# Expert layers of a two-layer trunk: where the third split buffer starts, and when the first expert blocks are split

## The chip, the cores and the metric

The kernel runs on one core of one Trainium2 chip. The metric is device time in microseconds (us) of one execution; lower is better. A core has TensorE (PE, matrix products), VectorE (DVE), ScalarE (ACT) and GpSimd (POOL), each with a queue of its own that it works through in order, and SyncE (SP), which only issues transfers here. Engines wait for each other through semaphores alone.

## The reference, cut to what matters

Two layers run over 640 tokens (128 of a prompt, 512 of a sample) of width 1024. Each layer has a mixer and then an expert stage, and the expert stage is where the change lies:

```python
q = (xc @ w_q).reshape(PEER_CHUNK, PEER_HEADS, 2, half)
s = jnp.einsum('thpc,hpnc->thpn', q, sub_keys)
sv, si = lax.top_k(s, PEER_TOPK)                  # 16 of 128, per token, head and half
cand = sv[..., 0, :, None] + sv[..., 1, None, :]
fv, fi = lax.top_k(cand.reshape(...), PEER_TOPK)  # 16 of the sums
gates = jax.nn.softmax(fv, axis=-1)
act = jax.nn.gelu(jnp.einsum('thkd,td->thk', u[eidx], xc))
y = jnp.einsum('thk,thkd->td', gates * act, v[eidx])
```

There are 16384 experts, so `u` and `v` are 16384 x 1024 each. For the sample the kernel doesn't gather: it computes all the products with `u`, and multiplies by a dense matrix of gates, and then all the products with `v`.

## The kernel before, in words

**Products in three passes.** A float32 product is made of three matmuls on rounded operands: with `hi` the rounded operand and `lo` the rest, hi·hi, hi·lo and lo·hi. The activations are split once (`hh`, `hl`). Each weight tile, 128 x 1024, is loaded to `wr` (`w_load`, line 277, on SP; 3 buffers), its high half `wh` is rounded on ScalarE (`w_hi`, line 294), and its low half `wl` is the difference, on line 303 (`w_lo`), on VectorE, or on GpSimd for tiles marked "g". `mm3` (line 361) issues the matmuls; with the order of `PAIRS`, the third matmul of a block is the first that reads `wl`.

**The order of the weights.** `seq` lists all weight tiles in the order of their use; for a layer's expert stage these are 16 query tiles `w_q` ("g"), 128 blocks of `u` and 128 blocks of `v` (both "v"). `w_get(ahead)` (line 341) hands out the next tile. Before that it splits tiles until `ahead` tiles from this one on are split, and asks for loads up to three further on:

```python
while st["split"] < min(i + ahead, len(seq)):
    w_split()
while st["load"] < min(i + 1 + AHEAD, len(seq)):
    w_load()
```

What stands in these loops goes into the queues of ScalarE, VectorE (or GpSimd) and SP at that point of the program; there is no other scheduler in the stretches that the change touches.

**Buffers of split tiles.** `wh` and `wl` have two buffers each (`WB`). `EXTRA` names tiles that go elsewhere: the third to fifth query tile, counted from 0 the tiles 2 to 4, have their own, and every third tile from 18 on (that is, from block 2 of `u`) takes a third buffer, `wh3` and `wl3` (lines 1267 to 1269). A split waits until the matmuls that read its buffer's former tile are done.

**The query chunks.** `peer` (line 1258) first plans the normalisation with the products of chunks 0 to 2 (`plan.run`, line 1368). Chunks 3 to 15 are a loop written out by hand (lines 1377 to 1387): `w_get()` with `ahead=2`, 48 matmuls of 320 columns, a copy of the result on ScalarE, and `score(c - 1)` for the chunk before: five matmuls against the keys on TensorE (line 1327), two copies on ScalarE (lines 1335 and 1333), and five calls of `top16` on VectorE (lines 1189 to 1193; called a search below), one for each 128 tokens. `s5` has 3 buffers, `q` has 2. `score(15)` ends the stage. Tile 16, which is block 0 of `u`, is split by the `w_get` of chunk 15.

**The blocks of `u`.** The loop from line 1532 runs over 128 blocks: `w_get(3)`, 24 matmuls of 512 columns into a new PSUM bank (`pu_`), a Gelu on ScalarE and a store. The rest of the routing goes between the blocks, step by step: `background()` (line 1429) yields its cost, and the loop spends a credit on it that grows by 4.6 a block:

```python
credit = min(credit + 4.6, 6.0)
while credit > 0 and alive:
    cst = next(bg, None)
```

The credit starts at -10. The steps are the second top-16, the softmax, one-hot operands for groups of four tokens (lines 1464 and 1466) and their matmuls (lines 1410 and 1411). From the prompt's routing on each block also takes one product of a gathered row with the prompt (`dot`, line 1397), and two when the background is through. When it is, and nothing of it is on its way, other pools open (`open_late`, line 1481); then each block takes a step of layer 1's modulation (line 189; in layer 0 only, 96 steps), and eight blocks each load a part of the dense gates (line 1504).

**The blocks of `v`.** The loop from line 1603 runs over 128 blocks, 24 matmuls each (line 1618), with one gathered row added for the prompt (line 1596), and modulation steps in five of eight blocks.

Of the kernel before, what the change touches and what calls it, by code (L numbers as in the profile page):

```python
# [28 lines left out]
NB = 128  # L29
# [127 lines left out]
def tile_trunk(ctx: ExitStack, tc: tile.TileContext, a, o):  # L157
# [110 lines left out]
    st = {"load": 0, "split": 0, "get": 0}  # L268
# [3 lines left out]
    def w_load():  # L272
        i = st["load"]
        if i < len(seq):
            ap, K, M, _ = seq[i]
            r = pw.tile([128, 1024], F32, name="wr", tag="wr", bufs=3)
            SP.dma_start(r[:, :K * M], ap if K == 1 else ap.rearrange("p k m -> p (k m)"))
            RAW[i] = r
            st["load"] += 1

    def w_hi():
        i = st["split"]
        while st["load"] <= i:
            w_load()
        _, K, M, eng = seq[i]
        n = K * M
        if i in EXTRA:
            hi, lo = EXTRA.pop(i)
            if callable(hi):
                hi, lo = hi(), lo()  # L290
        else:
            hi = pw.tile([128, 1024], F32R, name="wh", tag="wh", bufs=WB)
            lo = pw.tile([128, 1024], F32R, name="wl", tag="wl", bufs=WB)
        S.activation(hi[:, :n], RAW[i][:, :n], AF.Copy)  # L294
        SPLIT[i] = (hi, lo)
        st["split"] += 1
        return i

    def w_lo(i, eng=None):
        _, K, M, e = seq[i]  # L300
        n = K * M
        hi, lo = SPLIT[i]
        (eng or (V if e == "v" else G)).tensor_tensor(lo[:, :n], RAW.pop(i)[:, :n], hi[:, :n],  # L303
                                                      op=OP.subtract)

    def w_split():
        if st["split"] < len(seq):
            w_lo(w_hi())
# [32 lines left out]
    def w_get(ahead=2):  # L341
        i = st["get"]
        st["get"] += 1
# [4 lines that stand above are left out]
        _, K, M, _ = seq[i]  # L348
        hi, lo = SPLIT.pop(i)
        if K == 1:  # L350
            return hi, lo
        return (hi[:, :K * M].rearrange("p (k m) -> p k m", k=K),
                lo[:, :K * M].rearrange("p (k m) -> p k m", k=K))
# [3 lines left out]
    def mm3(outs, L, R, K, order=None):  # L357
        for i, k in enumerate(order or range(K)):
            for n, (x, y) in enumerate(PAIRS):
                for h, out in enumerate(outs):  # L360
                    PE.matmul(out, L[x](k), R[y](k, h), start=(i == 0 and n == 0),  # L361
                              stop=(i == K - 1 and n == 2))
# [10 lines left out]
    def wcol(t):  # L373
        return lambda k: t[:, k, :]
# [811 lines left out]
    def top16(v16, ix, s5, c, tt):  # L1186
        sc = s5[:, tt]
        v, x = v16[:, tt, c], ix[:, tt, c]
        V.max(v[:, 0:8], sc)  # L1189
        V.max_index(x[:, 0:8], v[:, 0:8], sc)  # L1190
        V.match_replace(sc, v[:, 0:8], sc, -3e38)  # L1191
        V.max(v[:, 8:16], sc)  # L1192
        V.max_index(x[:, 8:16], v[:, 8:16], sc)  # L1193
# [64 lines left out]
    def peer(l, A, B, gt):  # L1258
        act_d = pd.tile([NB - NR, 128, TS], F32, name=f"act_d{l}")
        g_d = pd.tile([128, TS // GC, NB, GC], F32, name=f"g_d{l}")  # L1260
        with tc.tile_pool(name="pg", bufs=1) as pg:
# [2 lines left out]
            aP = pg.tile([128, 128], F32, name="aP")  # L1264
            idx = pg.tile([128, 128], I32, name="idx")
            gat = {}
            for i in range(st["get"] + 18, st["get"] + 16 + 2 * NB, 3):
                EXTRA[i] = tuple((lambda n=n: pg.tile([128, 1024], F32R, name=n, tag=n, bufs=1))
                                 for n in ("wh3", "wl3"))

# [16 lines left out]
            with tc.tile_pool(name="ph", bufs=1) as tmp, \  # L1287
# [29 lines left out]
                def copy_q(ps):  # L1317
                    q = tmp.tile([128, T], F32, name="q", tag="q", bufs=2)
                    S.activation(v2(q), ps[:, :, :HT], AF.Copy)
                    return q  # L1320

                def score_mm(c, s5, part):
                    q = qs[c]
                    pa = p_mm.tile([128, 512], F32, name="psa", tag="s", bufs=2)
                    for t in range(4 * part, 4 + part):
                        n = (t % 4) * 128
                        PE.matmul(pa[:, n:n + 128], q[:, t * 128:(t + 1) * 128], keys[:, c], start=True,
                                  stop=True)
                    return pa

                def score_copy(s5, part, pa):
                    if part:
                        S.activation(s5[:, 4], pa[:, :128], AF.Copy)
                    else:
                        S.activation(s5[:, 0:4], pa.rearrange("p (t n) -> p t n", t=4), AF.Copy)

                def s5_tile():
                    return tmp.tile([128, 5, 128], F32, name="s5", tag="s5", bufs=3)
# [31 lines left out]
                def score(c):  # L1370
                    s5 = s5_tile()
                    for part in range(2):
                        score_copy(s5, part, score_mm(c, s5, part))
                    for t in range(5):
                        top16(v16, ix, s5, c, t)

                for c in range(2, 16):
                    if c == 2:
                        ps = firsts[c][0]
                    else:  # L1380
                        hi, lo = w_get()
                        ps = p_mm.tile([128, 2, 512], F32, name="pp", tag="mm", bufs=3)
                        mm3([ps[:, h, :HT] for h in range(2)], (wcol(hi), wcol(lo)), RH, KD)
                    qs[c] = copy_q(ps)
                    if c > 2:
                        score(c - 1)
                score(15)

            pps = late.enter_context(tc.tile_pool(name="pps", bufs=1, space=PSUM))
# [82 lines left out]
                            yield "grp"  # L1472

            bg = background()
            credit = -10.0
            ndot = [0, False]
            alive = True
            opened = []
# [53 lines left out]
            for i in range(NB):  # L1532
                hi, lo = w_get(3)
# [19 lines left out]
                credit = min(credit + 4.6, 6.0)  # L1553
# [49 lines left out]
            for n in range(NB):  # L1603
                hi, lo = w_get(1)
# [55 lines left out]
    with tc.tile_pool(name="tmp", bufs=1) as tmp, tc.tile_pool(name="pmm", bufs=1, space=PSUM) as p_mm:  # L1660
# [146 lines left out]
        mixer0(p_mm, tmp, gt, firsts)  # L1807
    A, B, gt = norm_cols(0, 1)
    peer(0, A, B, gt)
    mod_finish(1, 0, 48)  # L1810
    A, B, gt = norm_cols(1, 0)
    with tc.tile_pool(name="tmp", bufs=1) as tmp, tc.tile_pool(name="pmm", bufs=1, space=PSUM) as p_mm:
        mixer1(p_mm, tmp, A, B, gt)
    A, B, gt = norm_cols(1, 1)
    peer(1, A, B, gt)
    with tc.tile_pool(name="tmp", bufs=1) as tmp, tc.tile_pool(name="pmm", bufs=1, space=PSUM) as p_mm:
        plan = Plan()
# [118 lines left out]
```

## Time and profile before

| what | us |
|---|---|
| median of 3 runs | 3701.89 |
| lowest and highest run | 3700.79, 3709.65 |
| the profiled execution | 3704.95 |
| its span in the trace | 3703.2 |
| TensorE busy in the span | 3581.9 |
| VectorE busy | 2976.3 |
| ScalarE busy | 1644.4 |
| GpSimd busy | 656.2 |

The profile is of one execution of the program; its times start at the first instruction. A row in order of time has the start, the duration, the engine, the line, the operation with the tile written and the tiles read, and, where the engine stood idle before it, for how long and what ended that. Rows of the waits sum such idle time by who waited for whom. The clock of a stretch is the share of TensorE's full clock (2.4 GHz) that was granted in it. A run of like instructions is put together in one row, with a count. The expert stage of layer 0 runs from about 358 to 1990 us, that of layer 1 from about 2056 us to the end of its blocks.

### The profile page before, as it was taken

What the parts mean: (1) busy time and instruction counts of PE and PEld (TensorE: products, weight loads), DVE (VectorE), ACT (ScalarE), POOL (GpSimd) and SP (SyncE); (2) the same over time, 40 slices, a digit from 0 to 9 for tenths busy, and PEclk for the clock granted to TensorE, in tenths of its full rate; (3) what the DMA queues carried; (4) which work ended last, traced back from release to release, by engine and by line L of the source; (5) the groups of instructions that cost most, each with busy time, mean ns of one, the idle gap of its engine ahead of it and who ended that gap; (6) DMA issues with size and microseconds to landing.
All of it is one profiled execution on the core that took longest, in us unless ns stands there. A gap on an engine that the chain in (4) does not pass through costs nothing. (4 is left out here: it accounts for less than half of the span.)

```text
span 3703.2 us, 52825 instructions
## 1 busy us (share of the span) xinstructions
PE 3581.9 (97%) x18190; PEld 2980.4 (80%) x18190; DVE 2976.3 (80%) x6989; ACT 1644.4 (44%) x2904; POOL 656.2 (18%) x564
## 2 busy tenths in 40 slices
PE   8998989999999999999996889999999999999998
PEld 6957978888888888888885888888888888888886
DVE  8967889898997788888887898998989656666665
ACT  6743324756757333333333423757657333333332
POOL 0000112111111322222210111111111412222220
PEclk9999999999999999999998999999999999999999
DMA  5243126888878999999991215878888978888883
GB/s 206 80 138 118 60 77 222 285 260 271 280 257 288 367 324 331 326 323 321 324 313 40 77 54 194 278 256 289 262 266 278 341 262 295 296 295 298 299 295 116
DMA packets 400162, 894.58 MB, mean 242 GB/s; under 512 B 33746, under 2 KB 170386, under 8 KB 399252
## 3 DMA queue, kind: packets, MB, share of 16 engines
q1 hardware_dynamic: 272884, 490.07, 41.3%
q0 software_dynamic: 74016, 271.09, 21.4%
q10 hardware_dynamic: 52992, 130.05, 9.0%
q8 instruction: 142, 2.33, 0.3%
q14 instruction: 128, 1.05, 0.1%
HBM read 758.26 MB, written 132.81 MB: 241 GB/s over the span
## 5 line engine op out<-in xcount | busy, mean ns | idle before, releaser
L303 DVE TENSOR_TENSOR wl<-wr,wh 128x1024 fp32r<-128x1024 f32 (+2 forms) x556 | 665.7, 1198 | 518.7 <-ACT wh L294 448.3
L294 ACT ACTIVATE wh<-wr 128x1024 fp32r<-128x1024 f32 (+1 forms) x578 | 601.8, 1042 | 930.7 <-PE po L1618 734.2
L1274 POOL DMA_INDIRECT gat<-in_u_dram,idx x256 | 289.1, 1129 | 1258.6 <-DVE oh L1464 642.8
L1618 PE MATMUL po<-wgl,wh 128*128 128x512 f32 x2032 | 501.8, 389 | 0.0
L1618 PE MATMUL po<-wgh,wh 128*128 128x512 f32 x2032 | 501.8, 389 | 0.0
L1618 PE MATMUL po<-wgh,wl 128*128 128x512 f32 x2032 | 501.8, 389 | 0.0
L1274 POOL DMA_INDIRECT gat<-in_v_dram,idx x256 | 303.6, 1186 | 1016.3 <-DVE accP L1596 957.4
L1618 PEld LDWEIGHTS po<-wgh,wl 128*128 128x128 f32 x2032 | 381.5, 188 | 79.1
L1618 PEld LDWEIGHTS po<-wgl,wh 128*128 128x128 f32 x2032 | 381.5, 188 | 79.1
L1618 PEld LDWEIGHTS po<-wgh,wh 128*128 128x128 f32 x2032 | 381.5, 188 | 79.1
L1596 DVE SCALAR_TENSOR_TENSOR accP<-gat,aP,accP 128x1024 f32<-128x1024 f32 x254 | 324.8, 1279 | 0.5
L1397 DVE SCALAR_TENSOR_TENSOR gat<-gat,hP 128x1024 f32<-128x1024 f32 x256 | 311.0, 1219 | 15.0 <-DMA gat<-in_u_dram,idx 14.9
L1466 DVE TENSOR_SCALAR oh<-iota,ij,gs 128x128 f16<-128x128 f16 x1024 | 322.0, 314 | 0.0
L1405 ACT ACTIVATE oh<-oh,gs 128x128 f16<-128x128 f16 x1024 | 316.5, 387 | 0.0
L1528 ACT ACTIVATE wgh<-w 128x512 fp32r<-128x512 f32 x256 | 161.9, 632 | 208.0 <-PE po L1618 205.8
L1464 DVE TENSOR_SCALAR oh<-iota,ij 128x128 f16<-128x128 f16 x1024 | 253.2, 247 | 0.0
L1530 DVE TENSOR_TENSOR wgl<-w,wgh 128x512 fp32r<-128x512 f32 x256 | 174.9, 683 | 8.7 <-ACT wgh L1528 8.7
L1417 ACT ACTIVATE stag<-pgm 128x512 f32<-128x512 f32 x256 | 135.5, 579 | 0.0
L1410 PE MATMUL pgm<-oh 128*128 128x128 f16 x1024 | 129.4, 220 | 0.0
L1411 PE MATMUL pgm<-oh 128*128 128x128 f16 x1024 | 128.1, 219 | 0.0
L189 DVE SCALAR_TENSOR_TENSOR mjunk<-wm,silu 128x1024 f16<-128x1024 f32 x96 | 117.0, 1218 | 11.0 <-DMA gt__12579<-g_d 9.1
L1410 PEld LDWEIGHTS <-oh 128*128 128x128 f16 x1024 | 96.9, 98 | 33.5 <-DVE oh L1464 23.3
(2260 smaller groups left out, 6989.3 us busy)
## 6 DMA issues: line engine op xcount, KB each, us to landing
wr<-in_uT_dram SPq DMA_DIRECT2D x256, 512.0 KB, 4.5
wr<-in_v_dram SPq DMA_DIRECT2D x256, 512.0 KB, 4.5
g_d<-stag ACTq DMA_DIRECT2D x128, 512.0 KB, 6.4
act_d<-at ACTq DMA_DIRECT2D x240, 256.0 KB, 4.8
at<-act_d SPq DMA_DIRECT2D x240, 256.0 KB, 4.8
wm<-in_w_mod_dram SPq DMA_DIRECT2D x88, 512.0 KB, 7.2
hl<-g_d SPq DMA_DIRECT2D x128, 256.0 KB, 5.6
wr<-in_w_q_dram SPq DMA_DIRECT2D x32, 512.0 KB, 3.6
```

Source lines behind the costliest of these rows:

```text
L294: S.activation(hi[:, :n], RAW[i][:, :n], AF.Copy)
L303: (eng or (V if e == "v" else G)).tensor_tensor(lo[:, :n], RAW.pop(i)[:, :n], hi[:, :n], op=OP.subtract)
L1274: G.indirect_dma_start(out=r, out_offset=None, in_=a[f"u{l}" if s < 128 else f"v{l}"], in_offset=bass.IndirectOffsetOnAxis(ap=idx[:, s % 1 ...
L1397: V.scalar_tensor_tensor(ug, ug, 1.0, hP, op0=OP.mult, op1=OP.mult, accum_out=aP[:, s:s + 1])
L1405: S.activation(oh[:, 2], oh[:, 1], AF.Copy, scale=gr[:, tl:tl + 1])
L1410: PE.matmul(pgm[:, n], oh[:, 0], oh[:, 1], start=True, stop=False)
L1464: V.tensor_scalar(oh[:, 0], iota16, ij[:, 1, tl:tl + 1], None, op0=OP.is_equal)
L1466: V.tensor_scalar(oh[:, 1], iota16, ij[:, 0, tl:tl + 1], gs[:, 0, tl:tl + 1], op0=OP.is_equal, op1=OP.mult)
L1528: S.activation(wh, w32, AF.Copy)
L1530: return lambda: V.tensor_tensor(wl, w32, wh, op=OP.subtract)
L1596: V.scalar_tensor_tensor(accP, vg, aP[:, s:s + 1], accP, op0=OP.mult, op1=OP.add)
L1618: PE.matmul(po[d], (hi, lo)[x][:, d * 128:(d + 1) * 128], (wh, wl)[y], start=(n == 0 and p == 0), stop=False)
```

## The change

The third buffer pair is used from tile 7 on, every third tile (7, 10, 13, then 16, which is block 0 of `u`, and so on), in place of from tile 18 on. The chunks' `w_get` keeps three tiles split from the one in use, in place of two. Ahead of `score(15)` a loop splits until three tiles beyond chunk 15 are split. The credit of the background work starts at -14.

```diff
-            for i in range(st["get"] + 18, st["get"] + 16 + 2 * NB, 3):
+            for i in range(st["get"] + 7, st["get"] + 16 + 2 * NB, 3):
                 EXTRA[i] = tuple((lambda n=n: pg.tile([128, 1024], F32R, name=n, tag=n, bufs=1))
                                  for n in ("wh3", "wl3"))
...
                     else:
-                        hi, lo = w_get()
+                        hi, lo = w_get(3)
                         ps = p_mm.tile([128, 2, 512], F32, name="pp", tag="mm", bufs=3)
...
                     if c > 2:
                         score(c - 1)
+                while st["split"] < st["get"] + 3:
+                    w_split()
                 score(15)
...
             bg = background()
-            credit = -10.0
+            credit = -14.0
```

## Rows read from the trace of the kernel before

**Rows 1.** TensorE in the page's first part: busy us, share of the span, instructions

```profile
PE 3581.9 (97%) x18190; PEld 2980.4 (80%) x18190; DVE 2976.3 (80%) x6989; ACT 1644.4 (44%) x2904; POOL 656.2 (18%) x564
```

**Rows 2.** waits of TensorE, whole span: us in total, times, longest

```profile
PE pu__20832 L361 <- DVE wl L303: 10.8, 1, 10.8
PE pu__4604 L361 <- DVE wl L303: 10.8, 1, 10.8
...
PE pu__20798 L361 <- DVE wl L303: 3.1, 1, 3.1
PE pu__4570 L361 <- DVE wl L303: 3.0, 1, 3.0
...
PE pt__21555 L1445 <- DVE fj L1255: 1.8, 1, 1.8
```

**Rows 3.** stretches, layer 0: busy per engine (instructions), clock, DMA share, GB/s

```profile
510.20:513.70 3.50, 3.50 (x10) 2.73 (x9) 3.22 (x17) 0.00 (x0) 0.00 (x0) 0.51 0.49 150
...
520.50:534.20 13.70, 6.13 (x15) 4.80 (x16) 9.27 (x33) 0.00 (x0) 0.00 (x0) 0.50 0.35 112
```

**Rows 4.** TensorE in order of time, layer 0: start us, us [idle before it <-releaser]

```profile
506.14 0.50 PE L361 MATMUL pu__4570<-hh,wh 128*128 128x512 f32 x1 [0.68 <-ACT s L1333]
...
509.89 0.51 PE L361 MATMUL pu__4570<-hh,wl 128*128 128x512 f32 x1 [3.02 <-DVE wl L303]
...
516.65 0.39 PE L361 MATMUL pu__4604<-hh,wh 128*128 128x512 f32 x1
...
528.07 0.80 PE L361 MATMUL pu__4604<-hh,wl 128*128 128x512 f32 x1 [10.81 <-DVE wl L303]
...
536.02 0.39 PE L361 MATMUL pu__4638<-hh,wh 128*128 128x512 f32 x1
...
541.47 0.39 PE L361 MATMUL pu__4692<-hh,wh 128*128 128x512 f32 x1
```

**Rows 5.** VectorE in order of time, same stretch

```profile
500.11 0.27 DVE L1189 MAX8 v<-s 128x8 f32<-128x128 f32 x1
...
508.63 1.21 DVE L303 TENSOR_TENSOR wl<-wr,wh 128x1024 fp32r<-128x1024 f32 x1
...
518.29 0.27 DVE L1189 MAX8 v<-s 128x8 f32<-128x128 f32 x1
...
526.81 3.48 DVE L303 TENSOR_TENSOR wl<-wr,wh 128x1024 fp32r<-128x1024 f32 x3
```

**Rows 6.** chain of waits, layer 1: start us, us, what

```profile
2318.76 5.47 PE pu__21602 L361 x24
```

**Rows 7.** ScalarE in order of time, layer 0

```profile
505.32 0.60 ACT L1335 ACTIVATE s<-psa 128x512 f32<-128x512 f32 x1 [1.13 <-issue]
...
505.97 2.00 ACT L294 ACTIVATE wh<-wr 128x1024 fp32r<-128x1024 f32 x2
```

**Rows 8.** SP's queue in order of time, layer 0

```profile
491.36 0.33 SPq L277 DMA_DIRECT2D wr<-in_uT_dram  x1
```

**Rows 9.** page's sixth part, DMA issues: count, size, us to landing

```profile
wr<-in_uT_dram SPq DMA_DIRECT2D x256, 512.0 KB, 4.5
```

**Rows 10.** VectorE in order of time, late blocks of layer 0

```profile
1211.47 1.22 DVE L189 SCALAR_TENSOR_TENSOR mjunk<-wm,silu 128x1024 f16<-128x1024 f32 x1 [9.12 <-DMA gt__12579<-g_d]
...
1212.62 1.22 DVE L303 TENSOR_TENSOR wl<-wr,wh 128x1024 fp32r<-128x1024 f32 x1
...
1271.31 1.22 DVE L303 TENSOR_TENSOR wl<-wr,wh 128x1024 fp32r<-128x1024 f32 x1
```

**Rows 11.** TensorE in order of time, late blocks of layer 0

```profile
1214.32 0.39 PE L361 MATMUL pu__12674<-hh,wl 128*128 128x512 f32 x1
```

**Rows 12.** all engines in order of time, chunk 13 of layer 0

```profile
480.78 2.40 POOL L303 TENSOR_TENSOR wl<-wr,wh 128x1024 fp32r<-128x1024 f32 x1 [5.74 <-ACT wh L294]
...
481.35 0.27 DVE L1189 MAX8 v<-s 128x8 f32<-128x128 f32 x1
...
483.06 0.27 DVE L1189 MAX8 v<-s 128x8 f32<-128x128 f32 x1
```

## The prediction, made before the changed kernel ran

> **What bounds the kernel now.** First the page's table of engines: TensorE is busy for 97% of the span, VectorE for 80% [rows 1]. So a gain has to come out of the few places where TensorE stands still. Second, the waits of TensorE over the whole span: four of its longer ones name the low half of an expert block, `wl` of line 303, a wait of 3.0 and one of 10.8 us in layer 0, and 3.1 and 10.8 us in layer 1 [rows 2]. They sit where the query chunks end and the expert blocks begin. Third, the granted clock there: from 510.2 to 513.7 it is 0.51 and from 520.5 to 534.2 it is 0.50 of full speed, so 1.2 in place of 2.4 GHz [rows 3]. It fell after TensorE had stood still in the first wait and while it stood still in the second, so each wait costs more than its length. Fourth, TensorE in order of time: block 0 starts at 506.14, its third matmul (the first that reads `wl`) only at 509.89; block 1 starts at 516.65 and its third matmul comes at 528.07; blocks 2 and 3 start at 536.02 and 541.47 [rows 4]. At full clock a block takes 541.47 - 536.02 = 5.45 us, its last 22 matmuls 5.00. From the third matmul to the end block 0 took 6.76 and block 1 7.95, so the lower clock cost 1.76 and 2.95. Fifth, what VectorE did meanwhile: it runs the top-16 searches without a pause and is late with them. The searches of chunk 13 begin at 500.11, the low half of block 0 follows at 508.63, then those of chunks 14 and 15 (the latter from 518.29), and only at 526.81 the low halves of blocks 1 to 3 [rows 5]. Five searches take 526.81 - 518.29 = 8.52, one low half 1.14 net (508.63 + 1.14 + 8.52 = 518.29), and TensorE resumes 1.26 after a low half starts (508.63 to 509.89, 526.81 to 528.07). The order of VectorE's queue sets the end here; TensorE needs 506.14 to 546.92 for four blocks that are 21.8 us of work.
>
> **The change, part by part, layer 0.** The two edits of `w_get(3)` and of the loop ahead of `score(15)` go together: on VectorE block 0's low half moves ahead of the searches of chunk 13, block 1's ahead of chunk 14's, block 2's ahead of chunk 15's. From 500.11 the queue then reads: low half 0 to 501.25, searches 13 to 509.77, low half 1 to 510.91, searches 14 to 519.43, low half 2 to 520.57, searches 15 to 529.09, low half 3. TensorE, unchanged up to 506.14: block 0 finds its low half there, and ends at 511.6; block 1 too, to 517.05. Block 2 issues two matmuls (0.45) and waits from 517.5 to 519.43 + 1.26 = 520.69, 3.2 us. That is the length of the wait at block 0 today, so I charge the same 1.76 of lower clock: it ends at 520.69 + 5.00 + 1.76 = 527.45. Block 3 issues two and waits from 527.9 to 529.09 + 1.26 = 530.35, 2.45 us. What this wait does to the clock no row of that length shows. From below it costs nothing: after a wait of 1.8 us for the transposes among layer 1's blocks [rows 2] the next block took 5.47 [rows 6]; from above 2.95, as after the 10.8 us. I take 1.76, the row it is nearest to in length. Block 3 ends at 530.35 + 5.00 + 1.76 = 537.1, against 541.47 + 5.45 = 546.92 today. **Gain 9.8 us**, between 8.6 (2.95 charged) and 11.6 (nothing). What the clock costs in block 2 hardly counts, since block 3 waits for VectorE anyhow.
>
> ScalarE: the rounding of block 2 (1.00, half of the pair at 505.97) is put ahead of the score copies of chunk 15. There ScalarE stands idle for 1.13 before 505.32, waiting for those scores [rows 7], so it costs nothing; without that cover the copies, and block 0 behind them, would start 1.0 later, which the 3.2 us wait of block 2 would take up. The roundings one chunk earlier fall into ScalarE's waits for the chunks' matmuls; each also writes a buffer whose chunk is done, the third buffer being what makes this so: with two, the rounding two ahead would have to wait for the chunk that is only now being issued. GpSimd's eleven low halves of query chunks start one chunk earlier in a queue that has nothing else then. Queued on SP are weight loads alone, in the same order; each waits for a low half that now comes earlier. Block 2's raw weights are asked for at 491.36 today [rows 8] and land 4.5 us later by the median [rows 9], at 495.9, with the change a chunk sooner; they are needed at 504.2. Its low half waits in VectorE's queue, ahead of chunk 15's searches, for a rounding that is done by 505.3 and which VectorE reaches at 519.43, so that nothing behind it is held up.
>
> The credit of -14: counted through the loop, the background work starts behind block 3 instead of 2, and each of its later steps one block later, the late pools opening at block 112 instead of 111. VectorE would otherwise have that work ahead of low halves that TensorE waits for. TensorE's one-hot matmuls are the same in number. The chunks of layer 1's modulation still run out in the last eight blocks: 16 steps in the first half and 80 in the second make the 96 that are needed (17 + 80 before). I cost it at nothing; the cover is VectorE's lead over TensorE, and it is thin at one place: at the opening VectorE stands 9.12 us for a load [rows 10], then delivers the low half from 1212.62 to 1213.84, and TensorE's first read of it is at 1214.32 [rows 11], 0.5 us of slack. If it comes 1 us later, 0.5 is paid there, and 1.76 of clock at most on top.
>
> The new phase of the third buffer in the expert blocks (every third from block 0, not from block 2) leaves three buffers in turn, as now: nothing.
>
> **Sum.** Layer 1 has the same waits within 0.1 us [rows 2], so 2 x 9.8 = 19.6 us. The profiled execution took 3704.95 (span 3703.2 and 1.75 around it), 3.06 above the median of the runs, 3701.89. So 3685.3 for it, and 3682.3 against the median.
>
> A rule is to be weighed here. While GpSimd's subtraction runs (480.78 to 483.18), two searches of VectorE begin 1.71 apart (481.35, 483.06) [rows 12]; with GpSimd idle it is 8.52 / 5 = 1.70 [rows 5]. So there is no stall, and the sum takes none. The Trainium skill's page "SBUF — State Buffer", section "SBUF: two separate sides", says that GpSimd shares a port pair with VectorE as an exclusive lock, against operations with two SBUF inputs or in a two-port mode. By that rule applied to searches the sum would be rival 4's; the trace speaks against it.
>
> **Rivals.** (1) The second wait of each layer costs no clock: 11.6 each, 3678.8. Its 2.45 us are shorter than any wait after which these rows show the clock falling, for it; for the forecast that 3.0 us did it twice. (2) The waits end in a long slow stretch as block 1 has it now: 8.6 each, 3684.7. Against it: 10.8 us of standing still came before that one. (3) Part is given back at the opening of the late pools, where the slack is 0.5: if VectorE comes there 5 us later in both layers, 4.5 and 1.76 are lost each time, 3682.3 + 12.5 = 3694.8, no change. Against it: everything there moves by one block together. (4) GpSimd's subtraction does stop the searches: one of the eleven leaves the stretch in which VectorE is late, which is 2.40 a layer more, 3677.5. (5) **Slower.** From the opening on VectorE needs (1271.31 - 1212.62) / 11 = 5.34 us a block [rows 10], TensorE 5.45: two products with gathered rows, and waits for those gathers. One block fewer is left to catch up in. If the gathers take 3 us more a block there, the twelve blocks become bound by VectorE at 8.3 us, 12 x 2.9 = 35 us a layer, 3682.3 + 70 = 3752. It decides from 5.45 us a block up, and outweighs the gain from 5.45 + 19.6 / 24 = 6.3. Against it: the number of those blocks and products stays the same. (6) That the change doesn't do what it says: the low halves go by program order, and only a late buffer could undo it; then nothing changes, 3702.
>
> **How the numbers follow.** About 0.3% (11 us) can be told from no change: faster is below 3690.8. Forecast 0.62, rival 1 0.13, rival 2 0.09, rival 3 0.06, rival 4 0.03, rival 5 0.04, rival 6 0.03. Faster: 0.62 + 0.13 + 0.09 + 0.03, and of rival 3 a third, where it is smaller: 0.89. Same 0.07, slower 0.04. The range takes in rivals 1, 2 and 4 with 1.5 us below for the bounds, and up to 3690 for a median that is drawn up as the runs before were (3700.79 to 3709.65) and for a partial rival 3: 3676 to 3690, leaving out about 0.15.
>
> **What would show it.** In the changed trace: no wait of block 0 and block 1 for `wl`; waits of about 3.2 and 2.45 us at blocks 2 and 3; the low halves of blocks 0 to 2 between the searches, and block 4 beginning 31 us after block 0 (40.8 now). The last search ends 2.3 us later than today. I am wrong if other waits for `wl` stand in the blocks, if the chunks take longer than now, or if block 4 comes as now.

## The result, and the profile after

The changed kernel takes 3682.93 us in the median of 5 runs (3677.67 to 3688.88); the kernel before took 3704.14 in 5 runs beside it (3700.79 to 3709.65). The ratio is 0.9944, with a 95% interval of 0.9931 to 0.9957: 21 us faster. The profiled execution took 3681.16 with a span of 3679.4, against 3704.95 and 3703.2, so the two traces differ by 23.8 us.

The first part of the page shows TensorE 5.6 us less busy and VectorE busy as before [rows 1]. About 3.1 of the 5.6 are the clock's: what the 22 matmuls behind each wait took beyond 5.00 us adds up to 9.2 before (1.76 and 2.95 in layer 0, 1.72 and 2.80 in layer 1) and to 6.1 now (1.45 and 1.70, 2.85 and 0.14). The rest is no more than two traces of one kernel differ by: a second trace of the changed kernel has 3571.7.

```profile
PE 3576.3 (97%) x18190; PEld 2974.7 (81%) x18190; DVE 2976.4 (81%) x6989; ACT 1644.5 (45%) x2904; POOL 658.0 (18%) x564
```

The waits of TensorE for the low halves (in total, times, longest) stand at other blocks now: `pu__4638` and `pu__20866` are block 2 of layer 0 and layer 1, `pu__4672` and `pu__20900` are block 3. They are 3.0 and 2.6 us in layer 0, and 3.0 and 1.2 in layer 1. The waits of 10.8 us [rows 2] are gone, and blocks 0 and 1 wait for no low half:

```profile
PE pu__20866 L361 <- DVE wl L303: 3.0, 1, 3.0
PE pu__4638 L361 <- DVE wl L303: 3.0, 1, 3.0
...
PE pu__4672 L361 <- DVE wl L303: 2.6, 1, 2.6
...
PE pu__20900 L361 <- DVE wl L303: 1.2, 1, 1.2
```

VectorE in order of time, layer 0 (start, duration; only the low halves are shown). One stands ahead of each chunk's searches, 9.68 us apart (497.58, 507.26, 516.93; that is 8.54 for five searches and 1.14 for a low half), and the fourth follows the last search at 526.60. In the kernel before there was one among them and three behind them [rows 5]:

```profile
497.58 1.20 DVE L303 TENSOR_TENSOR wl<-wr,wh 128x1024 fp32r<-128x1024 f32 x1
...
507.26 1.21 DVE L303 TENSOR_TENSOR wl<-wr,wh 128x1024 fp32r<-128x1024 f32 x1
...
516.93 1.21 DVE L303 TENSOR_TENSOR wl<-wr,wh 128x1024 fp32r<-128x1024 f32 x1
...
526.60 3.48 DVE L303 TENSOR_TENSOR wl<-wr,wh 128x1024 fp32r<-128x1024 f32 x3
```

TensorE in order of time, layer 0: the first matmul of blocks 0 to 4 (503.51, 509.13, 514.57, 524.64, 534.56), and for blocks 2 and 3 the third, the first that reads `wl`, with the wait ahead of it:

```profile
503.51 0.50 PE L361 MATMUL pu__4570<-hh,wh 128*128 128x512 f32 x1 [0.68 <-ACT s L1333]
...
509.13 0.39 PE L361 MATMUL pu__4604<-hh,wh 128*128 128x512 f32 x1
...
514.57 0.39 PE L361 MATMUL pu__4638<-hh,wh 128*128 128x512 f32 x1
...
518.19 0.80 PE L361 MATMUL pu__4638<-hh,wl 128*128 128x512 f32 x1 [3.01 <-DVE wl L303]
...
524.64 0.39 PE L361 MATMUL pu__4672<-hh,wh 128*128 128x512 f32 x1
...
527.86 0.80 PE L361 MATMUL pu__4672<-hh,wl 128*128 128x512 f32 x1 [2.61 <-DVE wl L303]
...
534.56 0.39 PE L361 MATMUL pu__4731<-hh,wh 128*128 128x512 f32 x1
```

Block 4 starts 31.05 us after block 0; it was 40.77 [rows 4, with 5.44 for the block behind the last row]. The granted clock of this stretch (the third number from the end of a row) is at half speed twice, from 517.6, while TensorE still waits, to 521.0, and from 527.8 to 531.3: 3.4 and 3.5 us, where before it was once for 3.5 and once for 13.7 us [rows 3]:

```profile
517.60:521.00 3.40, 2.81 (x7) 2.26 (x8) 3.16 (x15) 0.00 (x0) 0.00 (x0) 0.50 0.45 147
521.00:527.80 6.80, 4.25 (x19) 3.16 (x17) 6.35 (x29) 1.65 (x2) 0.00 (x0) 1.00 0.11 43
527.80:531.30 3.50, 3.44 (x8) 2.76 (x9) 3.47 (x8) 0.00 (x0) 0.00 (x0) 0.51 0.63 187
531.30:540.00 8.70, 8.70 (x39) 7.16 (x39) 6.86 (x36) 1.66 (x2) 0.00 (x0) 1.00 0.46 157
```

ScalarE: the rounding of block 2 stands in the gap ahead of the score copies of chunk 15. Of the 1.13 us that ScalarE stood idle there [rows 7], 0.18 is left, and the copies are not later for it: they start 1.24 us after the first of the score matmuls whose result they copy, as before (501.45 to 502.69, and 504.08 to 505.32):

```profile
501.45 1.06 ACT L294 ACTIVATE wh<-wr 128x1024 fp32r<-128x1024 f32 x1
502.69 0.60 ACT L1335 ACTIVATE s<-psa 128x512 f32<-128x512 f32 x1 [0.18 <-ACT wh L294]
```

**Where the 23.8 us come from**, by the starts of blocks 0 and 4 in the two traces: 9.72 in layer 0's stretch (40.77 to 31.05) and 11.20 in layer 1's (40.69 to 29.49). Up to block 0 of layer 0 the new trace is 2.63 ahead (506.14 to 503.51); 0.31 lie between the two stretches, and behind the second it is 0.06 slower. The 2.63 are not the change's: from the stage's first score matmul to block 0 each of the two traces takes 123.1 us (383.05 to 506.14, and 380.40 to 503.51), so they arise ahead of the change, and in a second trace of the changed kernel block 0 starts at 499.12.

### The profile page after: what moved, and what is told of

Same layout as the page of the kernel before. It is cut to its first block, busy times and chain, and to the rows that moved or that the text cites. A ratio compares the mean times of both kernels' runs of the same rounds, so it can differ in the third digit from the quotient of the medians.

```text
span 3679.4 us, 52832 instructions
## 1 busy us (share of the span) xinstructions
PE 3576.3 (97%) x18190; PEld 2974.7 (81%) x18190; DVE 2976.4 (81%) x6989; ACT 1644.5 (45%) x2904; POOL 658.0 (18%) x564
```

## Experiments

**The credit, taken back.** On the changed kernel:

```diff
-            credit = -14.0
+            credit = -10.0
```

> The changed kernel with the credit back at -10, all else kept. Theory (the order of VectorE's queue around the last searches makes the gain, the credit makes none): the background starts behind block 2 again, 5.6 us of it stand ahead of the low half of block 5, which is then done at about 538 where TensorE reads it at 543 (times of the kernel before); no new wait, the same time as the changed kernel within 2 us (about 3682 where before has 3704), and the small waits late in layer 0's blocks (0.3 and 0.5 us) are gone. Rival (the later start of the background is part of the gain): a wait for wl at block 5 or 6 of 2 us or more and a slow stretch after it in each layer, 4 to 10 us slower than the changed kernel.

Measured: 3683.56 us, ratio to the kernel before 0.9939 (0.9926 to 0.9952). That is the changed kernel's time (the intervals overlap). No wait for `wl` stands at blocks 4 to 6, so the later start of the background pays for nothing. But waits of 0.2 and 0.3 us late in layer 0 stayed, against the theory: the credit doesn't cause those. The trace shows something else as well. TensorE in order of time in layer 1, third matmul of block 2, first of block 3, third of block 3, first of block 4:

```profile
2206.97 0.50 PE L361 MATMUL pu__20866<-hh,wl 128*128 128x512 f32 x1 [3.04 <-DVE wl L303]
...
2212.13 0.39 PE L361 MATMUL pu__20920<-hh,wh 128*128 128x512 f32 x1
...
2216.64 0.79 PE L361 MATMUL pu__20920<-hh,wl 128*128 128x512 f32 x1 [3.89 <-DVE wl L303]
...
2224.64 0.39 PE L361 MATMUL pu__20969<-hh,wh 128*128 128x512 f32 x1
```

After the wait of 3.04 us block 2's last 22 matmuls took 2212.13 - 2206.97 = 5.16, hardly more than the 5.00 at full clock, and the clock of that stretch is 1.00 of full speed (2.4 GHz); after the next wait, of 3.89 us, it is 0.50 for 6.8 us and the 22 matmuls took 8.00:

```profile
2207.00:2212.10 5.10, 5.10 (x22) 4.21 (x23) 4.69 (x25) 0.00 (x0) 0.00 (x0) 1.00 0.36 108
...
2216.00:2222.80 6.80, 6.16 (x15) 4.80 (x16) 6.49 (x23) 0.00 (x0) 0.00 (x0) 0.50 0.49 154
```

**The credit alone.** On the kernel before:

```diff
-            credit = -10.0
+            credit = -14.0
```

> The kernel before with the credit at -14 alone. Theory: the four waits for wl at blocks 0 and 1 stay as they are (3.0 and 10.8 us, 3.1 and 10.8 us); 0 to 1.5 us slower than before, by waits late in layer 0's blocks like those of the changed kernel. Rival (credit is part of the gain): 4 us or more faster than before.

Measured: 3705.96 us, ratio 1.0002 (0.9994 to 1.0011). Same time, same waits (of layer 0, in the rows):

```profile
PE pu__4604 L361 <- DVE wl L303: 10.9, 1, 10.9
...
PE pu__4570 L361 <- DVE wl L303: 3.1, 1, 3.1
```

**Without the loop ahead of the last score.** On the changed kernel:

```diff
-                while st["split"] < st["get"] + 3:
-                    w_split()
                 score(15)
```

> The changed kernel without the loop ahead of the last score, so that block 2's low half comes after the searches of chunk 15 and those of blocks 0 and 1 stay ahead. Theory: no wait at blocks 0 and 1; block 2 waits for the end of all searches, on the scale of the kernel before from 517.5 to 527.95 + 1.26 = 529.2, 11.7 us, and then has the 2.95 us of lower clock; block 3 has no wait; block 4 comes 36.5 us after block 0 (40.8 before, 31.0 and 29.5 in the changed kernel): 4.3 us gained per layer, 8.6 in all, 3695 where before has 3704. Rival (it is the number of buffers and of tiles split ahead that counts, one low half more or less does not): as the changed kernel, 3682.

Measured: 3696.81 us, ratio 0.9972 (0.9963 to 0.9981), against 3705.77 for the kernel before on the same chip: 9.0 us, and 8.6 were expected. Two low halves stand between the searches and three behind them, on VectorE in order of time:

```profile
501.26 1.21 DVE L303 TENSOR_TENSOR wl<-wr,wh 128x1024 fp32r<-128x1024 f32 x1
...
510.93 1.21 DVE L303 TENSOR_TENSOR wl<-wr,wh 128x1024 fp32r<-128x1024 f32 x1
...
529.12 3.48 DVE L303 TENSOR_TENSOR wl<-wr,wh 128x1024 fp32r<-128x1024 f32 x3
```

TensorE now waits at block 2 for all that is ahead of the third:

```profile
PE pu__20866 L361 <- DVE wl L303: 11.6, 1, 11.6
PE pu__4638 L361 <- DVE wl L303: 11.5, 1, 11.5
```

Block 4 starts 35.70 us after block 0 in layer 0 and 36.61 in layer 1, where 36.5 was expected: behind its wait of 11.5 us layer 0 lost 2.07 to the clock, layer 1 2.95. So the number of tiles split ahead counts only by which low half stands ahead of which searches; the loop, two lines, makes more than half of the gain (9 of the 21 us are left without it). Neither the loop without `w_get(3)` nor `w_get(3)` without the third buffer from tile 7 was run, so how these share the rest is not shown.

**The low halves of the first blocks on GpSimd.** On the changed kernel:

```diff
-        add_seq(f"uT{l}", NB, 8, 128, "v")
+        add_seq(f"uT{l}", range(6), 8, 128, "g")
+        add_seq(f"uT{l}", range(6, NB), 8, 128, "v")
```

> The changed kernel with the low halves of blocks 0 to 5 of each layer on GpSimd in place of VectorE. Theory (what is left of the waits is VectorE's queue alone): GpSimd needs 2.4 us for one, a block 5.45, so no block waits for wl; blocks 0 to 3 take 21.8 us and block 4 comes 21.9 us after block 0 in both layers (31.05 and 29.5 in the changed kernel); the last search ends 3.4 us earlier; 9.2 + 7.6 = 16.8 us faster than the changed kernel, about 3666 where before has 3704. Rival one (GpSimd's subtraction holds up the searches, as with one port for both): searches 2.4 us longer for each low half beside them, visible in the spacing of the searches, but still no wait for wl; the background then starts some 5 us late. Rival two (the waits are for loads of raw weights or for rounding): waits of 2 to 3 us stay at blocks 2 and 3, and the time is that of the changed kernel.

Measured: 3666.52 us, ratio 0.9893 (0.9879 to 0.9907). No block waits for `wl` at the start. GpSimd in order of time: the low halves of blocks 2, 3 and 4 (lines are one further in this file), each waiting only for its rounding:

```profile
505.04 2.38 POOL L304 TENSOR_TENSOR wl<-wr,wh 128x1024 fp32r<-128x1024 f32 x1 [5.74 <-ACT wh L295]
515.29 2.39 POOL L304 TENSOR_TENSOR wl<-wr,wh 128x1024 fp32r<-128x1024 f32 x1 [7.87 <-ACT wh L295]
519.38 2.40 POOL L304 TENSOR_TENSOR wl<-wr,wh 128x1024 fp32r<-128x1024 f32 x1 [1.70 <-ACT wh L295]
```

TensorE, first matmuls of blocks 0 and 4: 21.89 us apart, and the same in layer 1, with no stretch of lower clock in either:

```profile
505.97 0.50 PE L362 MATMUL pu__4570<-hh,wh 128*128 128x512 f32 x1 [0.68 <-ACT s L1334]
...
527.86 0.39 PE L362 MATMUL pu__4731<-hh,wh 128*128 128x512 f32 x1
```

The last search starts its last step 19.47 us after block 0 begins, where it was 22.89 in the changed kernel: 3.42 less, which is the three low halves (1.14 each) that are gone from among the searches, and nothing of 2.4 us has come for any low half on GpSimd. So GpSimd's subtraction does not hold up the searches, and rival 4 falls. The rule of the Trainium skill's page "SBUF — State Buffer", section "SBUF: two separate sides", names operations with two SBUF inputs or in a two-port mode; by this trace these searches are not among them.

One other operation of VectorE was held up by GpSimd: the cast behind the last search. It began while a subtraction ran on GpSimd and took 1.55 us in layer 0 (1.52 in layer 1), until just behind the subtraction's end at 527.22; the same cast took 0.29 in the changed kernel, where GpSimd stood idle. TensorE did not wait for it. GpSimd and VectorE in order of time:

```profile
524.82 2.40 POOL L304 TENSOR_TENSOR wl<-wr,wh 128x1024 fp32r<-128x1024 f32 x1 [3.03 <-ACT wh L295]
...
525.82 1.55 DVE L1199 CAST ixf<-ix 128x256 f16<-128x256 uint32 x1
```

**The new phase of the third buffer alone.** On the kernel before:

```diff
-            for i in range(st["get"] + 18, st["get"] + 16 + 2 * NB, 3):
+            for i in range(st["get"] + 16, st["get"] + 16 + 2 * NB, 3):
```

> The kernel before with the third buffer on every third tile from 16 (block 0) in place of 18 (block 2), which gives the expert blocks the phase of the changed kernel without anything split earlier. Theory: three buffers in turn either way, so the four waits for wl stay (3.0 and 10.8 us per layer) and the time is that of before within 1.5 us. Rival (the phase itself is part of the gain, or brings the waits of 0.2 to 0.5 us late in layer 0's blocks): 3 us or more off, or such waits between blocks 111 and 127 of layer 0 together with a time 1 to 2 us above before.

Measured: 3700.02 us, ratio 0.9995 (0.9986 to 1.0005): no difference that can be told. The medians lie 3.3 us apart, at the rival's 3 us, so the time alone would not decide; the trace does: it has the waits of before, 3.1 and 10.8 us in layer 0 and 3.1 and 11.0 in layer 1, and block 4 comes 40.85 and 40.55 us after block 0.

**GpSimd without the change.** The kernel before with the two `add_seq` lines of the fourth experiment and nothing else:

> The kernel before with the low halves of blocks 0 to 5 of each layer on GpSimd, and nothing of the change. Theory (the order of VectorE's queue is all that made TensorE wait): on the scale of the kernel before, block 0's low half is done at about 499.3 on GpSimd, those of blocks 1 and 2 at 509.4 and 511.8, where TensorE reads them at 506.8, 512.0 and 517.5; no wait for wl, block 4 comes 21.9 us after block 0 in both layers, 37.8 us gained, 3667 to 3668 where before has 3705, as with both edits. Rival (two tiles split ahead of chunk 15 and the third buffer are needed as well): waits of 1 us or more at blocks 1 or 2 with a slow stretch after them, 2 to 5 us per layer slower than with both edits, 3671 to 3677.

Measured: 3665.32 us, ratio 0.9903 (0.9889 to 0.9918), against 3703.35 for the kernel before on the same chip: 38.0 us, and 37.8 were expected. GpSimd in order of time: block 0's low half at 490.79; those of blocks 1 and 2 as one run from 500.83, done by 505.59; block 3's at 509.23:

```profile
490.79 2.40 POOL L304 TENSOR_TENSOR wl<-wr,wh 128x1024 fp32r<-128x1024 f32 x1 [5.74 <-ACT wh L295]
500.83 4.76 POOL L304 TENSOR_TENSOR wl<-wr,wh 128x1024 fp32r<-128x1024 f32 x2 [7.64 <-ACT wh L295]
509.23 2.40 POOL L304 TENSOR_TENSOR wl<-wr,wh 128x1024 fp32r<-128x1024 f32 x1 [3.63 <-ACT wh L295]
```

TensorE: the first matmuls of blocks 0 and 1, the third of block 1 (no wait ahead of it) and the first of block 4, 21.93 us after block 0:

```profile
499.86 0.50 PE L362 MATMUL pu__4570<-hh,wh 128*128 128x512 f32 x1 [0.68 <-ACT s L1334]
...
505.47 0.39 PE L362 MATMUL pu__4604<-hh,wh 128*128 128x512 f32 x1
...
505.93 0.39 PE L362 MATMUL pu__4604<-hh,wl 128*128 128x512 f32 x1
...
521.79 0.39 PE L362 MATMUL pu__4741<-hh,wh 128*128 128x512 f32 x1
```

This beats both kernels, and with the change added it is not told apart from it (the intervals overlap): neither the third buffer from tile 7 nor three tiles split ahead of the chunks are needed once the low halves are out of VectorE's queue.

**The changed kernel once more**, for its trace:

> The changed kernel once more, for its trace. Theory (the two waits of a layer are set by VectorE's queue, what the lower clock adds to them is not set by the kernel): waits of 3.0 us at block 2 in both layers, the last search 22.9 us after block 0 begins, and block 4 anywhere from 27.9 (no clock lost) to 34 us after block 0, not the same in the two layers (31.05 and 29.5 in the first trace). Rival (each wait costs its fixed 1.76 us): 31.0 in both layers.

Measured: one run, 3676.57 us. The waits are 2.9 us at block 2 in both layers, 2.6 at block 3 in layer 0 and 1.2 in layer 1; block 4 comes 30.92 and 29.39 us after block 0:

```profile
PE pu__20866 L361 <- DVE wl L303: 2.9, 1, 2.9
PE pu__4638 L361 <- DVE wl L303: 2.9, 1, 2.9
...
PE pu__4672 L361 <- DVE wl L303: 2.6, 1, 2.6
...
PE pu__20900 L361 <- DVE wl L303: 1.2, 1, 1.2
```

So the two layers differ again, and nearly by the same as in the first trace; a fixed cost of 1.76 a wait is refuted. The theory left the clock's part open, for anything from 27.9 to 34 us; it came as in the first trace, within 0.04 us at each of the four waits: 1.49 and 1.72 in layer 0 (1.45 and 1.70 there), 2.88 and 0.13 in layer 1 (2.85 and 0.14). Two traces are few, but they do not bear out that the kernel has no part in it.

## Why the prediction was right

**The time: nearer than its working earns.** 3682.3 was forecast and 3682.93 came. But the forecast took 19.6 off 3701.89, and the kernel before had 3704.14 beside the changed one, with a gain of 21.2. That these two differences nearly cancel is luck. The gain in the two stretches, 9.72 + 11.20 = 20.9, is 1.3 above the 19.6 of the sum.

**VectorE's queue: right, to tenths.** On the scale of block 0's start, low half 3 was predicted 22.95 us after it (529.09 - 506.14) and came 23.09 after (526.60 - 503.51). Block 2's wait was to be 3.2 us and is 3.0. Block 3's third matmul was to come 24.2 us after block 0's start; it came 24.35 after in layer 0 (527.86 - 503.51) and 24.35 after in layer 1 (2211.08 - 2186.73), although the layers lost unlike amounts of clock before. That bears out that the clock in block 2 hardly counts. The third and the fourth experiment show the cause: one low half put back behind the searches brought block 4 later by 4.7 us in layer 0 (35.70 against 31.05) and 7.1 in layer 1 (36.61 against 29.49); with all of them off VectorE it came at 21.89.

**The clock: right for layer 0, charged too much in layer 1.** Each wait was charged 1.76, and the charge of the second wait is the one that enters the sum. Layer 0 lost 1.45 (524.64 - 518.19 - 5.00) and 1.70 (534.56 - 527.86 - 5.00). In layer 1 the first wait cost 2.85 and the second 0.14. TensorE there in order of time, first matmul of block 0, third of block 2, first and third of block 3, first of block 4:

```profile
2186.73 0.50 PE L361 MATMUL pu__20798<-hh,wh 128*128 128x512 f32 x1 [0.68 <-ACT s L1333]
...
2201.41 0.80 PE L361 MATMUL pu__20866<-hh,wl 128*128 128x512 f32 x1 [3.02 <-DVE wl L303]
...
2209.26 0.40 PE L361 MATMUL pu__20900<-hh,wh 128*128 128x512 f32 x1
...
2211.08 0.50 PE L361 MATMUL pu__20900<-hh,wl 128*128 128x512 f32 x1 [1.19 <-DVE wl L303]
...
2216.22 0.39 PE L361 MATMUL pu__20959<-hh,wh 128*128 128x512 f32 x1
```

and its clock in two stretches, the first from while TensorE stood still until 2207.2:

```profile
2200.40:2207.20 6.80, 5.79 (x14) 4.53 (x15) 6.32 (x30) 0.00 (x0) 0.00 (x0) 0.50 0.24 81
2207.20:2216.20 9.00, 7.81 (x34) 6.09 (x33) 8.59 (x30) 1.66 (x2) 0.00 (x0) 1.00 0.52 150
```

The long slow block 2 left only 1.2 us to wait at block 3, after which the clock did not fall. So layer 1 gave 11.2 in place of 9.8, near the upper bound of 11.6, as in rival 1, though by another way than rival 1 had it: not a wait of 2.45 us that costs nothing, but a shorter one. Rival 2, a long stretch at the end, is what the first experiment's layer 1 had (8.00 - 5.00 = 3.00 lost after 3.89 us, block 4 after 32.34 us). Both rivals are thus real outcomes of single layers, though this last one gained 40.69 - 32.34 = 8.35, a little under the lower bound of 8.6.

**The edits costed at nothing** were nothing: the credit (first and second experiment) and the phase (fifth). Only the side remark on the credit, that background work would stand ahead of low halves that TensorE waits for, is not borne out: with -10 it stood there, and TensorE did not wait for them. ScalarE's 1.13 us did hold the rounding.

**Rivals 3 and 5.** At the opening of the late pools VectorE waited 9.1 us as before, and no long wait came of it. From block 4 to block 127 layer 0 took 738.35 us in the new trace and 737.69 in the old one; the other traces lie from 737.75 to 738.86, those without the new credit and those without the new phase among them. So what is lost there is 0.1 to 1.2 us and not the change's; where it comes from stays open. Rival 5's stretch stayed within TensorE's pace (from 1205.74 to 1264.54 eleven low halves, 5.35 us each, against 5.45 a block), rival 6 is excluded by the order in the trace.

## What to carry to other kernels

Where an engine that does side work feeds the busiest one, look at the stage borders: what the next stage needs first stands behind the backlog of the old one in an in-order queue, and its price is the backlog, once a border. Ask first whether that work can go to an engine with nothing to do there: here another engine's mark on six tiles of each layer gave 38 us, where reordering with more buffers gave 21, since every low half that stays in the late queue still pushes the searches back. Look also at what else the two engines do side by side: here one cast was held for 1.3 us. A wait's clock cost can be bounded from rows (0 to 2.95 here, exceeded by 0.05), but not taken as fixed.

## What the runs showed of the hardware that was not expected

The clock after a wait of the same length is not the same. After waits of 2.9 to 3.1 us the 22 matmuls that follow lost 1.45 (layer 0, changed kernel), 2.85 (layer 1, changed kernel), 1.76 (block 0, kernel before [rows 4]) and 0.16 us (layer 1, first experiment, clock 1.00 throughout). In the changed kernel's second trace the two layers repeat theirs (1.49 and 2.88), so it is not all chance. Nor does the loss simply grow with the wait: it was 3.00 after 3.9 us (layer 1, first experiment) and 2.07 after 11.5 (layer 0, third experiment). What decides between these was not tried.

GpSimd's subtractions of 2.40 us held up a cast of VectorE, 1.55 us in place of 0.29 (fourth experiment; 1.70 in layer 0 of the sixth), and not its searches, which began every 1.70 or 1.71 us beside them.
